# A decoder layer on one core: block sums loaded a tile ahead of their making, residual tiles loaded one a row block, half rows' statistics taken early

## The chip, the cores and the metric

The kernel runs on one core of a Trainium2 chip. The metric is the device time of one execution in microseconds (us). Each kernel is executed several times and the median counts. A profile is one further execution under the hardware profiler; its times are read from the start of its span.

Engines are named as in the profile: PE is the matrix engine (PEld its weight loads), DVE the vector engine, ACT the scalar engine, POOL GpSimd, SP SyncE, which here only issues DMAs. Each engine works through its own queue of instructions in order. In the listings of the timeline, a row is: start in us, duration in us, engine, source line, operation, destination and sources, count, and in brackets the idle time ahead of it with the instruction that ended that idle time.

## The reference, cut to what matters

One layer of a hybrid decoder in float32, for 1024 rows of width 1024. Two SwiGLU feed-forward networks (FFN1 and FFN2, hidden width 2816) stand around a token mixer. The change lies in the two feed-forward networks and their layer norms alone.

```python
def layer_norm(x, g, b, eps=LN_EPS):
    xf = x.astype(jnp.float32)
    mu = jnp.mean(xf, axis=-1, keepdims=True)
    var = jnp.mean(jnp.square(xf - mu), axis=-1, keepdims=True)
    return ((xf - mu) * lax.rsqrt(var + eps) * g + b).astype(x.dtype)

def swiglu(x, w_gate, w_up, w_down):
    return (jax.nn.silu(x @ w_gate) * (x @ w_up)) @ w_down

...
x = layer_norm(ALPHA * x + 0.5 * swiglu(x, ffn1_w_gate, ffn1_w_up, ffn1_w_down), ln1_g, ln1_b)
x = layer_norm(ALPHA * x + token_mixer(x, ...), ln2_g, ln2_b)
x = layer_norm(ALPHA * x + 0.5 * swiglu(x, ffn2_w_gate, ffn2_w_up, ffn2_w_down), ln3_g, ln3_b)
```

## The kernel before

**Arithmetic.** Every float32 operand of a product is split into a high and a low part (`split`: ACT casts the high part, L134, and POOL or DVE subtracts to get the low part, L138), and a product of 128x128 by 128x512 is three matmuls on PE: high by high, high by low, low by high (`mm3`, L154). The 2x2 block products of the feed-forward networks go by a scheme of seven products in place of eight.

**The gate half.** A loop over f = 0 to 21 (`gate_rest`) takes 128 columns of the gate and up weights at a time. One block is seven products of 12 matmuls of width 512; between them DVE adds the results (L291 and others) and the hidden rows h are stored to DRAM.

**Block sums.** The down half also needs sums and differences of quarters of its two operands. `sums` makes them ahead, in the gate loop: four 128x512 tiles are loaded (L388) into a ring of four buffers named `pr`, four additions or subtractions on DVE follow (L390 to L393 for kind "h", quarters of the hidden rows; L396 to L399 for kind "w", quarters of w_down), and the four results go to DRAM (L402). The blocks f = 0 to 10 each make one "w" sum, the blocks f = 12 to 21 one "h" sum, and `down_seven` makes the last "h" sum at its start.

**The down half.** `down_seven` runs seven products m = 0 to 6 of 11 row blocks i. For each block `part_load` (L418) loads two 128x512 tiles into a ring of eight buffers `rw`, both are split into a ring of fourteen buffers `wr` (here DVE makes the low parts), and PE runs 12 matmuls: three for each of four accumulators j. Products m = 0, 2, 3, 4 gather in the PSUM banks c, c, a, d, products 1, 5, 6 in g, g, b, b. At the end of product 0 DVE scales the residual tiles and adds the accumulators (12 instructions, L461); later products add theirs (L466). The eight residual tiles `u` (128x1024, from x or from x2) are loaded at block 3 of product 0 (L447), all at one place, right behind `hooks[0]`, which loads the layer norm's gain and bias (`lng`, `lnb`, L194). After product 4 the layer norms of row tiles 0 to 3 are handed out over the following blocks, and those of tiles 4 to 7 come after product 6. `layer_norm` takes two `bn_stats` a tile (L523, one for each half of the row), then an aggregate, a scale and a shift.

**What sets the order.** The order on each engine's queue is not that of the program text: a list scheduler places instructions at build time, with the program's order as the priority and the rings' buffers as limits. A load into a ring waits until the buffer's last reader is done; for `pr` this is the store at L402.

Of the kernel before, what the change touches and what calls it, by code (L numbers as in the profile page):

```python
# [16 lines left out]
P = 128  # L17
# [5 lines left out]
NH = NF // 2  # L23
# [8 lines left out]
class Net:  # L32
    def __init__(self, ctx, tc, ins, out):
        self.ctx, self.tc, self.nc, self.I, self.out = ctx, tc, tc.nc, ins, out
        tp = lambda **kw: ctx.enter_context(tc.tile_pool(**kw))
        self.cp = tp(name="cp", bufs=1)
        self.gp = {}
        self.sp = self.rp = self.ep = self.wp = None
        self.pp = tp(name="pp", bufs=1, space=PSUM)
        self.dp = tp(name="dp", bufs=1, space=bass.MemoryType.DRAM)  # L40
        self.n = 0
        self.SD = {}


    def nm(self, s):
# [280 lines left out]
    def gate_first(self, pre, src, cmb, hD):  # L326

        nc = self.nc
# [15 lines left out]
        for _ in steps:  # L344
            pass
        self.gate_up(cmb, 0, ws, hD, 256, 512)
        self.sums(pre, "w", self.I[f"{pre}_w_down"][0], 0)
        return self.gate_rest(pre, cmb, hD, 1)

    def gate_rest(self, pre, cmb, hD, f0):  # L350

        wd = self.I[f"{pre}_w_down"][0]
        for f in range(f0, NF):
            ws = self.weights(*(self.raws(pre, f, 0) + self.raws(pre, f, 1)))
            if f == NF - 1:
                self.down_parts(pre, hD)
                ahead = [self.part_load(0, i) for i in range(2)]
            if f == 0:
                self.gate_up(cmb, f, ws, hD, 0, 256)
                self.gate_up(cmb, f, ws, hD, 256, 512)  # L360
            else:
                self.gate_up(cmb, f, ws, hD)
            if f < NH:
                self.sums(pre, "w", wd, f)
            elif f > NH:
                self.sums(pre, "h", hD, f - NH - 1)
        return ahead


# [6 lines left out]
            r, c = c, r  # L376
        return src[(r * NH + i) * P:(r * NH + i + 1) * P, c * 512:(c + 1) * 512]

    def sums(self, pre, kind, src, i):

        nc = self.nc
        tt_ = nc.vector.tensor_tensor
        key = pre + kind
        if key not in self.SD:
            self.SD[key] = self.dram("sum_" + key, 4 * NH * P, 512)
        q11, q12, q21, q22 = (self.ring("pr") for _ in range(4))
        for t, r, c in ((q11, 0, 0), (q12, 0, 1), (q21, 1, 0), (q22, 1, 1)):
            nc.sync.dma_start(t, self.quarter(src, kind, r, c, i))  # L388
        if kind == "h":
            tt_(q22, q21, q22, op=ALU.add)  # L390
            tt_(q21, q11, q21, op=ALU.subtract)  # L391
# [29 lines left out]
    def down_seven(self, pre, src, hD, ln_cb, hooks, ahead):  # L421

        nc = self.nc
        stt, tt_ = nc.vector.scalar_tensor_tensor, nc.vector.tensor_tensor
        y, late, ahead = [], [], list(ahead)
        self.sums(pre, "h", hD, NH - 1)
        acc = {}
        for m in range(7):
            name = "XYXZZYY"[m]
# [4 lines left out]
            for i in range(NH):  # L434
# [4 lines left out]
                for t in raws:  # L439
                    d = self.ring("wr"), self.ring("wr")  # L440
                    self.split(t, *d, lo_eng="dve")
                    ds.append(d)
                if (m, i) == (0, 3):
                    hooks[0]()
                    for tt in range(8):
                        t = self.unit()
                        nc.sync.dma_start(t, src[tt * P:(tt + 1) * P, :])  # L447
                        y.append(t)
                if (m, i) == (5, 0):
                    hooks[1]()  # L450
                if i % 5 == 4 and late:
                    late.pop(0)()
                for j in range(4):
# [2 lines left out]
            for j in range(4):  # L456
# [5 lines left out]
                elif m == 2:  # L462
                    stt(c11, c11, ALPHA, ps[j], op0=ALU.mult, op1=ALU.add)
                else:
                    t = {1: c12, 3: c22, 4: c12, 5: c22, 6: c21}[m]
                    tt_(t, t, ps[j], op=ALU.add)  # L466
                if m == 4:
                    late.append(lambda tt=j: ln_cb(tt, y))
        for j in range(4):
# [46 lines left out]
    def layer_norm(self, tt, y, gb, bb, then):  # L516

        nc = self.nc
        if tt % 2 == 0:
            self.mv = self.s("lnmv", [P, 2, 2], bufs=2)  # L520
        st = self.s("lnst", [P, 2, 6], bufs=2)
        for i in range(2):
            nc.vector.bn_stats(st[:, i], y[tt][:, i * 512:(i + 1) * 512])  # L523
        nc.vector.bn_aggr(self.mv[:, tt % 2], st)
        nb = self.s("lnn", [P, 1], bufs=2)
# [898 lines left out]
```

## Time and profile before

| | |
|---|---|
| median of 3 runs | 3321.55 us (3304.94 to 3331.37) |
| the profiled execution's own time | 3326.53 us |
| its span | 3324.7 us |
| DVE busy | 62% of the span |
| mean granted PE clock | 0.955 |

The span is from the first to the last instruction; 1.83 us of the profiled execution lie outside it. The profiled execution is 5 us longer than the median. On this time scale FFN1's gate half runs from about 24 to 505 us, its down half to 753, the mixer and its output product follow, FFN2's gate half runs from about 2570 to 3078, its down half to 3304, and the last layer norm and the stores of the output end the span.

### The profile page before, as it was taken

What the parts mean: (1) busy time and instruction counts of PE and PEld (TensorE: products, weight loads), DVE (VectorE), ACT (ScalarE), POOL (GpSimd) and SP (SyncE); (2) the same over time, 40 slices, a digit from 0 to 9 for tenths busy, and PEclk for the clock granted to TensorE, in tenths of its full rate; (3) what the DMA queues carried; (4) which work ended last, traced back from release to release, by engine and by line L of the source; (5) the groups of instructions that cost most, each with busy time, mean ns of one, the idle gap of its engine ahead of it and who ended that gap; (6) DMA issues with size and microseconds to landing.
All of it is one profiled execution on the core that took longest, in us unless ns stands there. A gap on an engine that the chain in (4) does not pass through costs nothing. (4 is left out here: it accounts for less than half of the span.)

```text
span 3324.7 us, 45401 instructions
## 1 busy us (share of the span) xinstructions
PE 3054.4 (92%) x15624; PEld 2474.3 (74%) x15624; DVE 2048.0 (62%) x4940; ACT 1067.3 (32%) x1750; POOL 778.6 (23%) x819
## 2 busy tenths in 40 slices
PE   7899897998899999999999999989999789989897
PEld 6687776876677777787877777767777678767686
DVE  8644554574647766757576766366649754455557
ACT  4232222453312222313132222276434323222343
POOL 4444430011212222222222122100000344443000
PEclk9999998999989999999999999999999799999999
DMA  6734556662222322322222232375586563455764
GB/s 217 244 93 129 168 162 228 193 207 76 59 61 62 79 74 58 78 63 73 65 73 68 74 87 78 106 233 162 173 265 203 191 216 87 128 162 175 243 197 159
DMA packets 535405, 454.55 MB, mean 137 GB/s; under 512 B 115165, under 2 KB 403079, under 8 KB 535175
## 3 DMA queue, kind: packets, MB, share of 16 engines
q1 hardware_dynamic: 526151, 438.02, 43.5%
q0 software_dynamic: 4608, 8.39, 0.9%
q10 hardware_dynamic: 4416, 5.24, 0.5%
q8 instruction: 123, 2.02, 0.3%
q14 instruction: 107, 0.88, 0.1%
HBM read 322.03 MB, written 129.50 MB: 136 GB/s over the span
## 5 line engine op out<-in xcount | busy, mean ns | idle before, releaser
L154 PE MATMUL psg<-xT,wf 128*128 128x512 f32 x2352 | 640.2, 408 | 2.2 <-ACT f L968 1.2
L154 PEld LDWEIGHTS psg<-xT,wf 128*128 128x128 f32 x2352 | 429.8, 192 | 79.2 <-ACT f L968 1.6
L134 ACT CAST wr<-rw 128x512 fp32r<-128x512 f32 x488 | 288.7, 621 | 521.9 <-PE psg L154 167.1
L138 DVE TENSOR_TENSOR wr<-rw,wr 128x512 fp32r<-128x512 f32 x356 | 237.2, 697 | 185.1 <-ACT wr L134 183.1
L154 PE MATMUL psb<-xq,wr 128*128 128x512 f32 (+1 forms) x1104 | 280.9, 406 | 63.8 <-DVE e L291 61.8
L138 POOL TENSOR_TENSOR wr<-tw,wr 128x512 fp32r<-128x512 f32 x176 | 242.9, 1382 | 356.5 <-ACT wr L134 348.4
L154 PE MATMUL psa<-xT,w 128*128 128x512 f32 x1200 | 317.8, 407 | 8.3 <-DVE pj L604 4.6
L154 PEld LDWEIGHTS psb<-xq,wr 128*128 128x128 f32 x1104 | 213.0, 201 | 119.9 <-DVE e L291 75.1
L138 POOL TENSOR_TENSOR wr<-rw,wr 128x512 fp32r<-128x512 f32 x132 | 180.3, 1368 | 423.3 <-ACT wr L134 417.7
L154 PE MATMUL psc<-xq,wr 128*128 128x512 f32 (+1 forms) x1104 | 262.8, 387 | 4.8 <-DVE e L291 4.8
L154 PEld LDWEIGHTS psa<-xT,w 128*128 128x128 f32 x1200 | 222.4, 191 | 59.4 <-DVE pj L604 9.4
L154 PEld LDWEIGHTS psc<-xq,wr 128*128 128x128 f32 x1104 | 206.9, 194 | 47.3 <-DVE e L291 4.4
L134 ACT CAST wr<-tw 128x512 fp32r<-128x512 f32 x176 | 109.1, 621 | 397.2 <-PE psb L154 304.6
L291 DVE TENSOR_TENSOR e<-psb,e 128x512 f32<-128x512 f32 (+1 forms) x138 | 91.7, 665 | 187.0 <-PE psb L154 187.0
L154 PE MATMUL psc<-wr,wr 128*128 128x512 f32 x624 | 164.4, 398 | 28.3 <-ACT wr L134 27.8
L138 POOL TENSOR_TENSOR w<-raw,w 128x512 fp32r<-128x512 f32 (+1 forms) x51 | 65.6, 1302 | 491.2 <-PE psb L154 246.2
L138 POOL TENSOR_TENSOR wf<-rawf,wf 128x512 fp32r<-128x512 f32 x98 | 130.3, 1345 | 164.2 <-ACT wf L134 138.8
L154 PEld LDWEIGHTS psc<-wr,wr 128*128 128x128 f32 x624 | 118.8, 191 | 55.9 <-ACT wr L134 29.1
L154 PE MATMUL psg<-wr,wr 128*128 128x512 f32 x540 | 144.3, 396 | 7.6 <-DVE wr L138 6.9
L882 POOL TENSOR_SCALAR S<-S,PC 128x128 f32<-128x128 f32 x120 | 80.5, 671 | 296.5 <-DVE S L884 188.8
L154 PE MATMUL psb<-wr,wr 128*128 128x512 f32 x540 | 143.9, 395 | 0.0
L134 ACT CAST wf<-rawf 128x512 fp32r<-128x512 f32 x122 | 73.4, 619 | 196.0 <-PE psg L154 117.0
(368 smaller groups left out, 5472.1 us busy)
## 6 DMA issues: line engine op xcount, KB each, us to landing
rawf<-in_w_in_dram SPq DMA_DIRECT2D x98, 256.0 KB, 3.1
rw<-in_ffn_w_gate_dram SPq DMA_DIRECT2D x88, 256.0 KB, 3.0
rw<-in_ffn_w_up_dram SPq DMA_DIRECT2D x88, 256.0 KB, 3.1
pr<-in_ffn_w_down_dram SPq DMA_DIRECT2D x88, 256.0 KB, 4.2
pr<-h SPq DMA_DIRECT2D x88, 256.0 KB, 3.7
h<-e SPq DMA_DIRECT2D x80, 256.0 KB, 2.8
rw<-h SPq DMA_DIRECT2D x66, 256.0 KB, 3.5
rw<-in_ffn_w_down_dram SPq DMA_DIRECT2D x66, 256.0 KB, 3.2
```

The costliest lines, as they stand in the source:

```text
L134: nc.scalar.copy(hi, src)
L138: eng.tensor_tensor(lo, src, hi.bitcast(F32), op=ALU.subtract)
L154: self.nc.tensor.matmul(out, a[u], b[v], start=first and i == 0, stop=last and i == 2, skip_group_check=more)
L291: add = lambda o, a, b: nc.vector.tensor_tensor(o, a[:, cs], b, op=ALU.add)
L882: nc.gpsimd.tensor_scalar(S1, S, pcn, None, op0=ALU.mult)
```

## The change

`sums` is cut in two: `sums_load` issues the four loads of a sum, `sums_make` does the additions and the stores. In the program's text a sum's making now stands one block behind its loads (`self.pend` carries it over). The last "h" sum is loaded at block 1 of product 0 and made at block 7. The eight residual tiles are loaded one a block, at blocks 2 to 9 of product 0. The loads of the layer norm's gain and bias move from product 0, block 3, to product 1, block 3. After product 5 DVE takes `bn_stats` of the right half rows of tiles 4 to 7, which are final there, and `layer_norm` later takes only the left halves of these. The ring for the statistics has 6 buffers in place of 2.

```diff
--- before.py
+++ after.py
@@ -39,7 +39,7 @@
         self.pp = tp(name="pp", bufs=1, space=PSUM)
         self.dp = tp(name="dp", bufs=1, space=bass.MemoryType.DRAM)
         self.n = 0
-        self.SD = {}
+        self.SD, self.early, self.pend = {}, {}, None
 
 
     def nm(self, s):
@@ -344,7 +344,7 @@
         for _ in steps:
             pass
         self.gate_up(cmb, 0, ws, hD, 256, 512)
-        self.sums(pre, "w", self.I[f"{pre}_w_down"][0], 0)
+        self.pend = self.sums_load(pre, "w", self.I[f"{pre}_w_down"][0], 0)
         return self.gate_rest(pre, cmb, hD, 1)
 
     def gate_rest(self, pre, cmb, hD, f0):
@@ -360,10 +360,13 @@
                 self.gate_up(cmb, f, ws, hD, 256, 512)
             else:
                 self.gate_up(cmb, f, ws, hD)
+            if self.pend:
+                self.sums_make(*self.pend)
+                self.pend = None
             if f < NH:
-                self.sums(pre, "w", wd, f)
+                self.pend = self.sums_load(pre, "w", wd, f)
             elif f > NH:
-                self.sums(pre, "h", hD, f - NH - 1)
+                self.pend = self.sums_load(pre, "h", hD, f - NH - 1)
         return ahead
 
 
@@ -376,16 +379,21 @@
             r, c = c, r
         return src[(r * NH + i) * P:(r * NH + i + 1) * P, c * 512:(c + 1) * 512]
 
-    def sums(self, pre, kind, src, i):
+    def sums_load(self, pre, kind, src, i):
+
+        ts = [self.ring("pr") for _ in range(4)]
+        for t, (r, c) in zip(ts, ((0, 0), (0, 1), (1, 0), (1, 1))):
+            self.nc.sync.dma_start(t, self.quarter(src, kind, r, c, i))
+        return pre, kind, i, ts
+
+    def sums_make(self, pre, kind, i, ts):
 
         nc = self.nc
         tt_ = nc.vector.tensor_tensor
         key = pre + kind
         if key not in self.SD:
             self.SD[key] = self.dram("sum_" + key, 4 * NH * P, 512)
-        q11, q12, q21, q22 = (self.ring("pr") for _ in range(4))
-        for t, r, c in ((q11, 0, 0), (q12, 0, 1), (q21, 1, 0), (q22, 1, 1)):
-            nc.sync.dma_start(t, self.quarter(src, kind, r, c, i))
+        q11, q12, q21, q22 = ts
         if kind == "h":
             tt_(q22, q21, q22, op=ALU.add)
             tt_(q21, q11, q21, op=ALU.subtract)
@@ -423,7 +431,6 @@
         nc = self.nc
         stt, tt_ = nc.vector.scalar_tensor_tensor, nc.vector.tensor_tensor
         y, late, ahead = [], [], list(ahead)
-        self.sums(pre, "h", hD, NH - 1)
         acc = {}
         for m in range(7):
             name = "XYXZZYY"[m]
@@ -440,14 +447,15 @@
                     d = self.ring("wr"), self.ring("wr")
                     self.split(t, *d, lo_eng="dve")
                     ds.append(d)
-                if (m, i) == (0, 3):
-                    hooks[0]()
-                    for tt in range(8):
-                        t = self.unit()
-                        nc.sync.dma_start(t, src[tt * P:(tt + 1) * P, :])
-                        y.append(t)
-                if (m, i) == (5, 0):
-                    hooks[1]()
+                if m == 0 and 2 <= i < 10:
+                    t = self.unit()
+                    nc.sync.dma_start(t, src[(i - 2) * P:(i - 1) * P, :])
+                    y.append(t)
+                if (m, i) in ((0, 1), (0, 7)):
+                    self.sums_make(*self.pend)
+                    self.pend = self.sums_load(pre, "h", hD, NH - 1) if i == 1 else None
+                if (m, i) in ((1, 3), (5, 0)):
+                    hooks[m // 5]()
                 if i % 5 == 4 and late:
                     late.pop(0)()
                 for j in range(4):
@@ -464,6 +472,9 @@
                 else:
                     t = {1: c12, 3: c22, 4: c12, 5: c22, 6: c21}[m]
                     tt_(t, t, ps[j], op=ALU.add)
+                if m == 5:
+                    self.early[4 + j] = self.s("lnst", [P, 2, 6], bufs=6)
+                    nc.vector.bn_stats(self.early[4 + j][:, 1], c22)
                 if m == 4:
                     late.append(lambda tt=j: ln_cb(tt, y))
         for j in range(4):
@@ -518,8 +529,11 @@
         nc = self.nc
         if tt % 2 == 0:
             self.mv = self.s("lnmv", [P, 2, 2], bufs=2)
-        st = self.s("lnst", [P, 2, 6], bufs=2)
-        for i in range(2):
+        st = self.early.pop(tt, None)
+        part = range(2) if st is None else range(1)
+        if st is None:
+            st = self.s("lnst", [P, 2, 6], bufs=self.UB - 2)
+        for i in part:
             nc.vector.bn_stats(st[:, i], y[tt][:, i * 512:(i + 1) * 512])
         nc.vector.bn_aggr(self.mv[:, tt % 2], st)
         nb = self.s("lnn", [P, 1], bufs=2)
```
Since a scheduler places the instructions, the engines' queues show what the change moves. Names carry a running number; `h_77` and `h_78` are the hidden rows in DRAM, `sum_ffn1h` and `sum_ffn2h` the sums made from them.

**The start of product 0.** SP's queue in FFN1, before, from the last stores of the last "h" sum on: the eight residual tiles `u`, then the two `rw` tiles of block 4.

```order
L402 DMA sum_ffn1h<-pr_4110 128x512
L402 DMA sum_ffn1h<-pr_4111 128x512
L447 DMA u_4210<-in_x_dram 128x1024
L447 DMA u_4212<-in_x_dram 128x1024
L447 DMA u_4214<-in_x_dram 128x1024
L447 DMA u_4216<-in_x_dram 128x1024
L447 DMA u_4218<-in_x_dram 128x1024
L447 DMA u_4220<-in_x_dram 128x1024
L447 DMA u_4222<-in_x_dram 128x1024
L447 DMA u_4224<-in_x_dram 128x1024
L418 DMA rw_4238<-h_77 128x512
L418 DMA rw_4239<-in_ffn_w_down_dram 128x512
```
After, the same stretch, behind the four `pr` loads of the last sum:

```order
L452 DMA u_4174<-in_x_dram 128x1024
L452 DMA u_4200<-in_x_dram 128x1024
L426 DMA rw_4214<-h_77 128x512
L426 DMA rw_4215<-in_ffn_w_down_dram 128x512
L452 DMA u_4226<-in_x_dram 128x1024
L426 DMA rw_4240<-h_77 128x512
L426 DMA rw_4241<-in_ffn_w_down_dram 128x512
L452 DMA u_4252<-in_x_dram 128x1024
L426 DMA rw_4266<-h_77 128x512
L426 DMA rw_4267<-in_ffn_w_down_dram 128x512
L452 DMA u_4278<-in_x_dram 128x1024
L426 DMA rw_4292<-h_77 128x512
```
The `rw` tiles of block 4 stand behind two residual tiles in place of eight, and those of blocks 5 to 7 follow in turn; the stores of the last sum have moved behind block 7's tiles, and `lng` and `lnb`, which stood ahead of the stores, to product 1. In FFN2 the tiles of blocks 2 to 7 are already loaded ahead of this. SP's queue before, from the last sum's stores on, with block 8's `rw` tiles last:

```order
L402 DMA sum_ffn2h<-pr_26622 128x512
L402 DMA sum_ffn2h<-pr_26624 128x512
L402 DMA sum_ffn2h<-pr_26623 128x512
L447 DMA u_26724<-x2D 128x1024
L447 DMA u_26726<-x2D 128x1024
L447 DMA u_26728<-x2D 128x1024
L447 DMA u_26730<-x2D 128x1024
L447 DMA u_26732<-x2D 128x1024
L447 DMA u_26734<-x2D 128x1024
L447 DMA u_26736<-x2D 128x1024
L418 DMA rw_26846<-h_78 128x512
L418 DMA rw_26847<-in_ffn_w_down_dram 128x512
```
After, the same stretch:

```order
L452 DMA u_26686<-x2D 128x1024
L452 DMA u_26712<-x2D 128x1024
L452 DMA u_26738<-x2D 128x1024
L452 DMA u_26764<-x2D 128x1024
L452 DMA u_26790<-x2D 128x1024
L452 DMA u_26816<-x2D 128x1024
L410 DMA sum_ffn2h<-pr_26657 128x512
L410 DMA sum_ffn2h<-pr_26654 128x512
L410 DMA sum_ffn2h<-pr_26656 128x512
L410 DMA sum_ffn2h<-pr_26655 128x512
L426 DMA rw_26838<-h_78 128x512
L426 DMA rw_26839<-in_ffn_w_down_dram 128x512
```
Six residual tiles now stand ahead of the four stores and two behind block 8's tiles; before, seven stood between the stores and block 8.

**The end of product 0.** DVE's queue in FFN2, before: the low parts of product 1's blocks 0 and 1 (L138), then the scaling of the residual tiles from product 0's accumulators.

```order
L138 TENSOR_TENSOR wr_26939<-rw_26934,wr_26938 128x512
L138 TENSOR_TENSOR wr_26943<-rw_26935,wr_26942 128x512
L138 TENSOR_TENSOR wr_26963<-rw_26958,wr_26962 128x512
L138 TENSOR_TENSOR wr_26967<-rw_26959,wr_26966 128x512
L461 SCALAR_TENSOR_TENSOR u_26722<-u_26722,psc_26638 128x512
L461 SCALAR_TENSOR_TENSOR u_26730<-u_26730,psc_26638 128x512 x2
L461 SCALAR_TENSOR_TENSOR u_26724<-u_26724,psc_26639 128x512
L461 SCALAR_TENSOR_TENSOR u_26732<-u_26732,psc_26639 128x512 x2
L461 SCALAR_TENSOR_TENSOR u_26726<-u_26726,psa_26640 128x512
L461 SCALAR_TENSOR_TENSOR u_26734<-u_26734,psa_26640 128x512 x2
L461 SCALAR_TENSOR_TENSOR u_26728<-u_26728,psd_26641 128x512
L461 SCALAR_TENSOR_TENSOR u_26736<-u_26736,psd_26641 128x512 x2
```
After, the same stretch (L469 is the former L461):

```order
L138 TENSOR_TENSOR wr_26935<-rw_26930,wr_26934 128x512
L469 SCALAR_TENSOR_TENSOR u_26686<-u_26686,psc_26614 128x512
L469 SCALAR_TENSOR_TENSOR u_26790<-u_26790,psc_26614 128x512 x2
L469 SCALAR_TENSOR_TENSOR u_26712<-u_26712,psc_26615 128x512
L469 SCALAR_TENSOR_TENSOR u_26816<-u_26816,psc_26615 128x512 x2
L469 SCALAR_TENSOR_TENSOR u_26738<-u_26738,psa_26616 128x512
L469 SCALAR_TENSOR_TENSOR u_26850<-u_26850,psa_26616 128x512 x2
L469 SCALAR_TENSOR_TENSOR u_26764<-u_26764,psd_26617 128x512
L469 SCALAR_TENSOR_TENSOR u_26876<-u_26876,psd_26617 128x512 x2
L138 TENSOR_TENSOR wr_26939<-rw_26931,wr_26938 128x512
L138 TENSOR_TENSOR wr_26959<-rw_26954,wr_26958 128x512
```
Only one of the four low parts still stands ahead of the scaling; the other operand of block 0 and both of block 1 come behind it. FFN1 has the same order after, and before had three ahead of the scaling. PE's queue at product 1's block 0, before:

```order
L154 MATMUL psg_26930<-wr_26942,wr_26938 128x512
L154 MATMUL psg_26930<-wr_26943,wr_26938 128x512
L154 MATMUL psg_26930<-wr_26942,wr_26939 128x512
L154 MATMUL psg_26931<-wr_26942,wr_26938 128x512
L154 MATMUL psg_26931<-wr_26943,wr_26938 128x512
L154 MATMUL psg_26931<-wr_26942,wr_26939 128x512
L154 MATMUL psb_26932<-wr_26942,wr_26938 128x512
L154 MATMUL psb_26932<-wr_26943,wr_26938 128x512
L154 MATMUL psb_26932<-wr_26942,wr_26939 128x512
L154 MATMUL psb_26933<-wr_26942,wr_26938 128x512
L154 MATMUL psb_26933<-wr_26943,wr_26938 128x512
L154 MATMUL psb_26933<-wr_26942,wr_26939 128x512
```
After:

```order
L154 MATMUL psg_26926<-wr_26938,wr_26934 128x512
L154 MATMUL psg_26927<-wr_26938,wr_26934 128x512
L154 MATMUL psb_26928<-wr_26938,wr_26934 128x512
L154 MATMUL psb_26929<-wr_26938,wr_26934 128x512
L154 MATMUL psg_26926<-wr_26939,wr_26934 128x512
L154 MATMUL psg_26926<-wr_26938,wr_26935 128x512
L154 MATMUL psg_26927<-wr_26939,wr_26934 128x512
L154 MATMUL psg_26927<-wr_26938,wr_26935 128x512
L154 MATMUL psb_26928<-wr_26939,wr_26934 128x512
L154 MATMUL psb_26928<-wr_26938,wr_26935 128x512
L154 MATMUL psb_26929<-wr_26939,wr_26934 128x512
L154 MATMUL psb_26929<-wr_26938,wr_26935 128x512
```
The four high-by-high matmuls of the block now go first, and the fifth needs `wr_26939`, the low part that DVE makes behind the scaling.

**The "w" sums.** DVE's queue in FFN2 at the fifth "w" sum (`e` are the gate half's additions), before:

```order
L291 TENSOR_TENSOR e_23185<-psb_23190,e_23182 128x512
L269 TENSOR_TENSOR tw_23480<-rw_23476,rw_23472 128x512
L396 TENSOR_TENSOR pr_23786<-pr_23787,pr_23786 128x512
L291 TENSOR_TENSOR e_23186<-psc_23191,e_23185 128x512
L269 TENSOR_TENSOR tw_23481<-rw_23474,tw_23479 128x512
L397 TENSOR_TENSOR pr_23787<-pr_23789,pr_23787 128x512
```
After (L404 is the former L396):

```order
L291 TENSOR_TENSOR e_23176<-psb_23181,e_23173 128x512
L269 TENSOR_TENSOR tw_23472<-rw_23468,rw_23464 128x512
L291 TENSOR_TENSOR e_23177<-psc_23182,e_23176 128x512
L404 TENSOR_TENSOR pr_23786<-pr_23787,pr_23786 128x512
L269 TENSOR_TENSOR tw_23473<-rw_23466,tw_23471 128x512
L291 TENSOR_TENSOR e_23178<-psb_23181,e_23173 128x512
```
One addition more (L291) stands ahead of the sum's first subtraction, whose tiles a DMA brings. Of the 22 "w" sums, 10 have moved back, past up to three such additions or up to five weight subtractions (L269), and 12 stand where they stood. Of the 22 "h" sums none has moved among the additions and weight subtractions of DVE, and SP's queue from block 12 to the last stores of the gate loop has the same order before and after, in both networks.

## The prediction

> **What bounds the kernel now.** I read the page's busy times first, then the waits, then PE in slices of 25 us, then the timeline of the slices in which PE stands.
>
> ```profile
> span 3324.7 us, 45401 instructions
> PE 3054.4 (92%) x15624; PEld 2474.3 (74%) x15624; DVE 2048.0 (62%) x4940; ACT 1067.3 (32%) x1750; POOL 778.6 (23%) x819
> ...
> 175.00:275.00 100.00, 100.00 (x443) 82.84 (x442) 40.93 (x57) 31.57 (x53) 47.79 (x37) 1.00 0.31 87
> 300.00:500.00 200.00, 181.88 (x763) 146.61 (x762) 107.83 (x134) 51.43 (x86) 80.69 (x59) 0.97 0.53 166
> 525.00:550.00 25.00, 15.44 (x56) 12.27 (x57) 9.02 (x14) 8.30 (x14) 0.00 (x0) 0.73 0.88 315
> 2860.00:3070.00 210.00, 190.05 (x794) 153.62 (x793) 110.61 (x135) 56.55 (x95) 84.69 (x63) 0.96 0.53 166
> 3100.00:3125.00 25.00, 13.03 (x48) 10.01 (x47) 10.01 (x16) 7.77 (x13) 0.00 (x0) 0.73 0.88 327
> ```
>
> PE bounds the kernel: between 175 and 275 us it is never idle, at full clock (the columns behind a window's length are the busy times of PE, PEld, DVE, ACT and POOL, then granted clock, DMA share and GB/s). So only what stops PE counts. It stops at the two seams between gate half and down half (9.6 and 12.0 us idle in 25, the DMA engines 88% busy), and in the "h" sum stretches: 200 − 181.88 = 18.1 us and 210 − 190.05 = 20.0 us idle. There the clock of 0.97 and 0.96 takes another 200 × 0.03 + 210 × 0.04 = 14 us, so about 52 us are lost in these two.
>
> The seam of FFN1, PE first, then SP's issues, then DVE:
>
> ```profile
> 508.21 0.50 PE L154 MATMUL psc<-wr,wr 128*128 128x512 f32 x1 [3.29 <-ACT wr L134]
> ...
> 521.14 0.84 PE L154 MATMUL psd<-wr,wr 128*128 128x512 f32 x3
> 534.56 3.23 PE L154 MATMUL psc<-wr,wr 128*128 128x512 f32 x6 [12.58 <-ACT wr L134]
> 537.59 1.48 PE L154 MATMUL psa<-wr,wr 128*128 128x512 f32 x3
> 538.87 1.39 PE L154 MATMUL psd<-wr,wr 128*128 128x512 f32 x3
> 540.10 1.55 PE L154 MATMUL psc<-wr,wr 128*128 128x512 f32 x6
> ...
> 556.46 1.52 PE L154 MATMUL psg<-wr,wr 128*128 128x512 f32 x6
> ...
> 562.89 1.24 PE L154 MATMUL psg<-wr,wr 128*128 128x512 f32 x4 [2.64 <-DVE wr L138]
> ...
> 590.98 1.52 PE L154 MATMUL psc<-wr,wr 128*128 128x512 f32 x6
> ...
> 510.30 0.43 SPq L194 DMA_DIRECT2D lng<-in_ln_g_dram  x1
> ...
> 518.93 4.08 SPq L447 DMA_DIRECT2D u<-in_x_dram  x8
> 523.13 0.63 SPq L418 DMA_DIRECT2D rw<-h  x1
> ...
> 515.19 0.69 DVE L390 TENSOR_TENSOR pr<-pr,pr 128x512 f32<-128x512 f32 x1 [3.81 <-issue]
> ...
> 554.98 3.67 DVE L461 SCALAR_TENSOR_TENSOR u<-u,psc 128x512 f32<-128x512 f32 x6
> 558.56 1.88 DVE L461 SCALAR_TENSOR_TENSOR u<-u,psa 128x512 f32<-128x512 f32 x3
> 560.35 1.88 DVE L461 SCALAR_TENSOR_TENSOR u<-u,psd 128x512 f32<-128x512 f32 x3
> 562.15 3.10 DVE L138 TENSOR_TENSOR wr<-rw,wr 128x512 fp32r<-128x512 f32 x5
> ```
>
> The reader sees a chain: SP waits for the last "h" sum to store it, issues eight residual tiles, and only then block 4's `rw`; PE stands 12.58 us, and the matmuls after the gap are slow: block 4 takes 540.10 − 534.56 = 5.54 us. The same in FFN2, at block 8:
>
> ```profile
> 3099.78 0.84 PE L154 MATMUL psd<-wr,wr 128*128 128x512 f32 x3
> 3112.59 3.23 PE L154 MATMUL psc<-wr,wr 128*128 128x512 f32 x6 [11.97 <-ACT wr L134]
> ...
> 3123.13 1.52 PE L154 MATMUL psg<-wr,wr 128*128 128x512 f32 x6
> 3124.49 1.52 PE L154 MATMUL psb<-wr,wr 128*128 128x512 f32 x6
> 3125.85 1.52 PE L154 MATMUL psg<-wr,wr 128*128 128x512 f32 x6
> ...
> 3153.88 1.52 PE L154 MATMUL psc<-wr,wr 128*128 128x512 f32 x6
> ...
> 3086.59 0.43 SPq L194 DMA_DIRECT2D lnb<-in_ln_b_dram  x1
> ...
> 3091.78 0.69 DVE L390 TENSOR_TENSOR pr<-pr,pr 128x512 f32<-128x512 f32 x1 [3.58 <-DMA pr<-h]
> ...
> 3097.43 3.99 SPq L447 DMA_DIRECT2D u<-x2D  x7
> 3101.52 0.51 SPq L418 DMA_DIRECT2D rw<-h  x1
> ```
>
> An undisturbed block is 3125.85 − 3123.13 = 2.72 us, so a product of 11 is 29.92 us.
>
> **The "h" stretches: 0.** The queues of SP and DVE there have the same order before and after, and `pr` still holds one sum: its next loads wait for the last stores. What is named as a load one tile ahead does not take place there.
>
> **Residual tiles, FFN1.** Block 3 ends at 521.14 + 0.84 = 521.98. Without a stall the seven blocks left would end at 541.0; product 0 ends at 556.46, so 15.4 us is the most to be had and 0 the least (all waits for data move, none goes). After, two tiles and block 4's `rw` are issued from 510.3 on: 1.05 + 0.52 MB, at 315 GB/s 5 us, so block 4 comes about in time. Before block 8 lie six tiles of 0.52 MB, ten `rw` and four sum stores of 0.26 MB: 3.15 + 2.62 + 1.05 = 6.8 MB, 21.7 us from 510.3, and some 2 us of the `pr` loads' rest: 534. With 1.3 us for cast and split and about 1 us to landing (both estimates from the first `rw` issue to PE's start, 523.13 to 534.56, which also held 4 MB of tiles) it starts at 536.5; PE would reach it at 521.98 + 4 × 2.72 = 532.9. A stall of 3.6 us and 2 us of slow clock put the end at 546.7: **−9.5** (rounded; 0 to −15.4).
>
> **Residual tiles, FFN2.** PE reaches block 8 at 3100.62; it starts at 3112.59. After, six tiles are issued ahead of the stores, right behind the last `pr` loads (from 3086.2, where `lng` stood), and so move while DVE still waits for its tiles at 3091.78. The stores and block 8's `rw` follow by 3098, with 1.05 + 0.52 MB left to move, 5 us, plus 2.3 us: 3105.3. With 1.8 us of slow clock and three blocks product 0 ends at 3115.2: **−7.9** (0 to −14.3, no stall at all).
>
> **The scaling ahead of the low parts: a new wait.** The 12 scalings take 562.15 − 554.98 = 7.2 us. Before, block 0 of product 1 had its low parts ahead of them. After, one low part of block 0 stands behind them: PE runs four matmuls, 0.9 us, and then waits. The first scaling can start when the sixth matmul of the last block is done, 1.1 us ahead of the product's end; so the low part is there 7.2 + 0.7 − 1.1 = 6.8 us into product 1, near 7.0 with the hand-over, and PE idles 6.1 us. The slow clock after it lies between the gap of 2.64 us (the 12 matmuls from 562.89 to block 2 ran some 1.75 us long) and that of 12.58 us (5.54 − 2.72 = 2.8): I take 2.0, so product 1 takes 38.0 us. It took 590.98 − 556.46 = 34.5 in FFN1 and 3153.88 − 3123.13 = 30.75 in FFN2: **+3.5** and **+7.3** (together between +5, if product 0's last block hides more, and +13).
>
> [...]
>
> **Statistics and layer norm.** By DVE's queue seven `bn_stats` run behind product 6 in FFN2 before, four after; two rows of that stretch:
>
> ```profile
> 3305.44 1.28 DVE L523 BATCH_NORM_STATS2 lnst<-u 128x6 f32<-128x512 f32 x2
> ...
> 3318.28 2.48 DVE L537 SCALAR_TENSOR_TENSOR u<-u,lnr,lnb 128x1024 f32<-128x1024 f32 x2
> ```
>
> DVE is the path there, at 0.6 us for one: 3 × 0.6 = 1.8 at most, **−1.5** in each network since ACT's shifts also wait; −3 in all (0 to −3.6). The early ones lie ahead of low parts at product 6's start, 4 × 0.6 = 2.4 us where a block lead of `wr` buffers covers; and the layer norms of tiles 2 and 3 come later there: **+1** (0 to +4). Gain and bias loads amid product 1, on a queue that then has slack: 0 (to +3).
>
> **The "w" sums.** Two of the waits that stop PE by a sum's tiles:
>
> ```profile
> 94.57 0.69 DVE L397 TENSOR_TENSOR pr<-pr,pr 128x512 f32<-128x512 f32 x1 [4.67 <-issue]
> ...
> 98.34 4.35 PE L154 MATMUL psb<-xq,wr 128*128 128x512 f32 x12 [3.75 <-DVE e L291]
> ...
> 2647.54 1.41 DVE L396 TENSOR_TENSOR pr<-pr,pr 128x512 f32<-128x512 f32 x1 [3.82 <-DMA pr<-in_ffn_w_down_dram]
> 2649.61 4.53 PE L154 MATMUL psc<-xq,wr 128*128 128x512 f32 x12 [3.03 <-DVE e L291]
> ```
>
> Both belong to sums that move behind the next addition. Idle 3.75 + 3.03, and slow clock 4.35 + 4.53 − 2 × 2.88 = 3.1 (12 matmuls at 0.24): 9.9 us at most. The tile's wait stays and can meet the next addition, so I take half: **−5** (+4 to −10).
>
> **Sum.** −9.5 − 7.9 + 3.5 + 7.3 − 3 + 1 − 5 = −13.6 us against the profiled execution's 3326.5, so 3313. That execution lies 5 us above the median of the runs, 3321.55; from the median the sum gives 3308. I forecast 3310.
>
> **Rivals.** *Slower:* the new wait at product 1 comes in any case (+10.8), but product 0 gains little. For it: in FFN2 six tiles go into the queue before the sum is made, so the `pr` tiles may land late, the stores hold SP, and block 8's `rw` waits again. Against it: at 3086.59 1 MB of gain and bias stood behind the same loads and DVE waited only 3.58 us. If both gains are lost, −3 + 1 − 5 + 10.8 = +4, and +9 if the "w" waits only move: 3326 to 3331 from the median. It decides where the two gains make less than 10.8 − 7 = 3.8 us.
>
> *The seams go entirely:* −15.4 − 14.3 + 10.8 − 3 + 1 − 10 = −31, so 3291. For it: the 315 GB/s are a mean, and some of it is stores; against it the 6.8 MB ahead of block 8 in FFN1.
>
> *The "h" waits go too,* as the change's words say: −52 more at most, near 3256 with the forecast's other terms. Only for it: a shift of the same queue by some us against the stores. Against it stands the unchanged order.
>
> *Nothing to be seen:* the parts cancel within 4 us, 3318 to 3325. For it: every gain here is a wait for data that the same DMA engines must bring.
>
> **Chances.** Forecast (3300 to 3317) 0.48, seams gone 0.16, "h" waits gone 0.06, nothing 0.15, slower 0.15. A measurement of this kernel tells about 1% from no change, 33 us; faster by more than that (under 3288.3) needs the "h" waits or a little over the seams: 0.06 + 0.04 = 0.10; slower by more (over 3354.8) has no mechanism here that reaches it: 0.03; within 1% 0.87. The range 3288 to 3329 leaves out the "h" case, the best of the seams and the worst of the slower case.
>
> **What would show it.** In the changed profile: block 4 of FFN1 without a long gap; a gap of 3 to 6 us at block 8 of each product 0; a gap near 6 us with a low part of DVE as its releaser 0.9 us into each product 1; waits of PE for L291 in the "h" stretches unchanged, near 38 us idle; four `bn_stats` in the tail. I am wrong if the gap in product 1 is missing, if a residual tile is late for the scaling, or if the "h" stretches get shorter by more than 10 us.

## The result, and the profile after

| | before | after |
|---|---|---|
| median of 15 runs | 3316.46 us (3304.32 to 3331.37) | 3295.53 us (3285.8 to 3313.7) |
| ratio of the times | | 0.9943, 95% interval 0.9925 to 0.9962 |
| the profiled execution's span | 3324.7 us | 3284.1 us |

The change is 0.6% faster: 18.9 us by the ratio (12.6 to 24.9). The two profiled executions, of 3326.5 and 3285.8 us, lie further apart than the medians, 40.6 us by their spans. 12.8 us of this lie between FFN1's last down product and FFN2's first gate block (1879.6 us before, 1866.8 after), where both kernels have the same instructions but for the early statistics in the first layer norm; in the other profiles below this stretch takes 1849 to 1876 us. So spans are not compared here, only stages.

All stage times come from the timeline's rows: a gate block by the product of its gated halves on DVE (L319), a down product from its first matmul to the next one's. Two numbers are FFN1 / FFN2, in us. The tail is from the end of PE's last matmul to the span's end. An undisturbed stretch of ten blocks is 190.4 us, an undisturbed product 29.92 us; where an edit moves DVE's own instructions, the marks of the blocks move with them by up to 3 us.

| kernel | blocks 1-10 | blocks 12-21 | product 0 | product 1 | products 5+6 | tail |
|---|---|---|---|---|---|---|
| before | 209.6 / 208.0 | 217.0 / 219.9 | 48.2 / 44.6 | 34.5 / 30.8 | 70.0 / 60.0 | 21.1 |
| after | 207.1 / 203.4 | 216.8 / 217.5 | 33.0 / 32.4 | 37.7 / 37.6 | 71.8 / 60.0 | 19.1 |
| e1 residual tiles only | 210.7 / 208.2 | 216.8 / 218.8 | 38.6 / 39.5 | 37.3 / 35.4 | 70.0 / 60.0 | 21.2 |
| e1b the same, gain and bias moved | 211.9 / 206.3 | 212.4 / 212.1 | 37.5 / 36.7 | 37.4 / 38.2 | 69.4 / 60.0 | 21.2 |
| e2 after without e1b's part | 208.4 / 203.1 | 217.3 / 218.4 | 44.5 / 40.8 | 34.5 / 30.7 | 72.2 / 60.0 | 19.1 |
| e4 early statistics only | 210.4 / 206.3 | 220.7 / 213.7 | 48.1 / 42.8 | 34.4 / 30.8 | 71.6 / 60.0 | 19.1 |
| e5 two blocks split first | 208.2 / 203.5 | 220.7 / 204.8 | 33.4 / 35.2 | 36.4 / 33.6 | 71.5 / 60.0 | 19.2 |
| e10 scaling handed out | 210.1 / 204.9 | 215.8 / 212.9 | 33.2 / 34.8 | 30.0 / 30.0 | 71.9 / 60.0 | 19.1 |
| e7 making held back | 189.4 / 188.9 | 190.7 / 190.4 | 34.2 / 36.5 | 38.1 / 37.6 | 72.0 / 60.0 | 20.0 |
| e12 e7 and e10 | 189.4 / 188.9 | 191.3 / 190.1 | 34.1 / 35.4 | 30.0 / 30.0 | 71.6 / 60.0 | 19.3 |
| e13 before, held in its block | 187.7 / 192.2 | 189.3 / 189.3 | 49.0 / 45.0 | 34.5 / 30.8 | 67.1 / 60.0 | 21.1 |

The seams after the change, PE's timeline, FFN1 and then FFN2:

```profile
504.92 3.30 PE L154 MATMUL psc<-wr,wr 128*128 128x512 f32 x6 [3.30 <-ACT wr L134]
...
529.78 0.62 PE L154 MATMUL psc<-wr,wr 128*128 128x512 f32 x2
...
537.94 0.62 PE L154 MATMUL psg<-wr,wr 128*128 128x512 f32 x2
538.39 0.61 PE L154 MATMUL psb<-wr,wr 128*128 128x512 f32 x2
544.70 2.07 PE L154 MATMUL psg<-wr,wr 128*128 128x512 f32 x4 [5.69 <-DVE wr L138]
...
575.61 1.52 PE L154 MATMUL psc<-wr,wr 128*128 128x512 f32 x6
...
3069.22 0.73 PE L154 MATMUL psc<-wr,wr 128*128 128x512 f32 x2 [2.06 <-ACT wr L134]
...
3077.51 0.62 PE L154 MATMUL psg<-wr,wr 128*128 128x512 f32 x2
...
3084.27 2.08 PE L154 MATMUL psg<-wr,wr 128*128 128x512 f32 x4 [5.69 <-DVE wr L138]
...
3115.15 1.52 PE L154 MATMUL psc<-wr,wr 128*128 128x512 f32 x6
```

The gaps of 12.6 and 12.0 us in product 0 are gone; 2.06 us at block 8 of FFN2 is what is left of them. In their place PE runs four matmuls of product 1 and stands 5.69 us in both networks. DVE's timeline of FFN1 shows for what, and SP's how the tiles now come:

```profile
536.78 3.67 DVE L469 SCALAR_TENSOR_TENSOR u<-u,psc 128x512 f32<-128x512 f32 x6 [0.53 <-PE psc L154]
540.37 1.88 DVE L469 SCALAR_TENSOR_TENSOR u<-u,psa 128x512 f32<-128x512 f32 x3
542.17 1.87 DVE L469 SCALAR_TENSOR_TENSOR u<-u,psd 128x512 f32<-128x512 f32 x3
543.96 3.09 DVE L138 TENSOR_TENSOR wr<-rw,wr 128x512 fp32r<-128x512 f32 x5
...
507.00 0.91 SPq L452 DMA_DIRECT2D u<-in_x_dram  x2
508.00 0.41 SPq L426 DMA_DIRECT2D rw<-h  x1
...
518.43 2.95 SPq L410 DMA_DIRECT2D sum_ffn1h<-pr  x4
522.40 0.32 SPq L426 DMA_DIRECT2D rw<-h  x1
```

The first low part of the five at 543.96 is the one that PE needs: it stands behind all 12 scalings. The lists of waits (total, times, longest) and two windows over the "h" blocks tell what has not changed. The waits before, then after:

```profile
PE psb L154 <- DVE e L291: 64.2, 32, 4.0
DVE pr L390 <- DMA pr<-h: 64.7, 21, 5.0
DVE pr L396 <- DMA pr<-in_ffn_w_down_dram: 37.3, 13, 5.3
...
PE psb L154 <- DVE e L291: 62.9, 34, 3.8
DVE pr L398 <- DMA pr<-h: 60.8, 21, 5.1
DVE pr L404 <- DMA pr<-in_ffn_w_down_dram: 43.1, 14, 5.1
```

The windows after, with the columns of the prediction's, which shows those before:

```profile
300.00:500.00 200.00, 182.78 (x774) 147.96 (x775) 105.91 (x132) 51.08 (x86) 78.63 (x58) 0.97 0.52 165
2825.00:3035.00 210.00, 191.84 (x804) 155.20 (x803) 112.53 (x138) 57.10 (x97) 87.28 (x65) 0.96 0.53 165
```

PE still stands 17 and 18 us in these windows, the clock is still 0.97 and 0.96, and DVE waits for the sums' tiles as long as before (104 us in these two rows, 102 before). A load one tile ahead did not come about in the gate loop.

### The profile page after: what moved, and what is told of

Same layout as the page of the kernel before. It is cut to its first block, busy times and chain, and to the rows that moved or that the text cites. A ratio compares the mean times of both kernels' runs of the same rounds, so it can differ in the third digit from the quotient of the medians.

```text
span 3284.1 us, 45405 instructions
## 1 busy us (share of the span) xinstructions
PE 3035.6 (92%) x15624; PEld 2456.9 (75%) x15624; DVE 2051.9 (62%) x4940; ACT 1066.5 (32%) x1750; POOL 779.6 (24%) x819
## 5 line engine op out<-in xcount | busy, mean ns | idle before, releaser
L138 DVE TENSOR_TENSOR wr<-rw,wr 128x512 fp32r<-128x512 f32 x356 | 238.0, 697 | 162.6 <-ACT wr L134 161.4
L138 POOL TENSOR_TENSOR wr<-tw,wr 128x512 fp32r<-128x512 f32 x176 | 243.1, 1382 | 353.9 <-ACT wr L134 348.2
L138 POOL TENSOR_TENSOR wr<-rw,wr 128x512 fp32r<-128x512 f32 x132 | 178.9, 1357 | 416.7 <-ACT wr L134 411.1
L291 DVE TENSOR_TENSOR e<-psb,e 128x512 f32<-128x512 f32 (+1 forms) x138 | 91.7, 664 | 184.1 <-PE psb L154 184.1
L138 POOL TENSOR_TENSOR w<-raw,w 128x512 fp32r<-128x512 f32 (+1 forms) x51 | 66.6, 1318 | 471.9 <-ACT w L134 410.7
L138 POOL TENSOR_TENSOR wf<-rawf,wf 128x512 fp32r<-128x512 f32 x98 | 131.3, 1355 | 164.9 <-ACT wf L134 150.0
```

The source lines that it names most:

```text
L138: eng.tensor_tensor(lo, src, hi.bitcast(F32), op=ALU.subtract)
L291: add = lambda o, a, b: nc.vector.tensor_tensor(o, a[:, cs], b, op=ALU.add)
```

## The experiments

**The residual tiles alone.** The kernel before, with the residual tiles spread (e1), then also with the gain and bias loads moved (e1b).

```diff
+                if m == 0 and 2 <= i < 10:
+                    t = self.unit()
+                    nc.sync.dma_start(t, src[(i - 2) * P:(i - 1) * P, :])
+                    y.append(t)
                 if (m, i) == (0, 3):
                     hooks[0]()
-                    for tt in range(8):
-                        t = self.unit()
-                        nc.sync.dma_start(t, src[tt * P:(tt + 1) * P, :])
-                        y.append(t)
```

In e1b `hooks[0]` runs at `(m, i) == (1, 3)`.

> The kernel before with one part of the change: the eight residual tiles are loaded one a block at blocks 2 to 9 of product 0 (gain and bias stay at block 3, sums and statistics as before). Theory (the spread of the residual tiles makes the gain, and itself moves the scaling ahead of product 1's low parts): product 0 falls from 48.2 to 36-39 us in FFN1 and from 44.6 to 33-36 in FFN2, product 1 rises to 37-38 in FFN1 and 33-35 in FFN2, in all 15 to 20 us less than before, ratio 0.994 to 0.9955. Rival (the gain needs the last sum to be made later, since its stores hold SP): product 0 of FFN1 stays over 44 us and the ratio over 0.997.

> The kernel before with the residual tiles spread and the loads of gain and bias moved to product 1 (sums and statistics as before). Theory (of the 5.5 to 7 us by which product 0 stays above the changed kernel when only the residual tiles are spread, the gain and bias loads ahead of block 4 or 8, 1 MB or some 2.6 us, are a part and the stores of the last sum ahead of the tiles the rest): product 0 at 35-37.5 us in both networks. Rival (gain and bias cost nothing there): 38.5 and 39.5 us as without them moved.

e1: ratio 0.9969 (0.9949 to 0.9988), less gain than the expected 0.994 to 0.9955, though the interval reaches into it; product 0 falls to 38.6 as expected and to 39.5, where 33 to 36 were expected; product 1 rises to 37.3 and 35.4. The rival, by which FFN1's product 0 stays over 44, falls. e1b, one run of 3288.28 us beside a median of 3308.64 for the kernel before: product 0 at 37.5 and 36.7, as its theory has it. SP's queue of e1 in FFN1 shows what is still ahead of block 4:

```profile
510.35 0.91 SPq L445 DMA_DIRECT2D u<-in_x_dram  x2
515.02 2.98 SPq L402 DMA_DIRECT2D sum_ffn1h<-pr  x4
518.04 0.43 SPq L194 DMA_DIRECT2D lng<-in_ln_g_dram  x1
518.52 0.46 SPq L194 DMA_DIRECT2D lnb<-in_ln_b_dram  x1
519.08 0.38 SPq L418 DMA_DIRECT2D rw<-h  x1
```

SP is ready at 511.3 and then waits 3.8 us for DVE to make the last sum, in order to store it. So product 0's gain has three parts, FFN1 / FFN2: the residual tiles 9.7 / 5.1 us (48.2 to 38.6, 44.6 to 39.5), gain and bias 1.1 / 2.8, and the last sum's stores behind the tiles 4.5 / 4.3 (37.5 to 33.0, 36.7 to 32.4). These are differences of single profiles, and part of each is slow clock: of the 4.5 us by which e1b's product 0 in FFN1 is longer than the changed kernel's only 1.5 are idle, and block 5 there takes 529.36 − 524.40 = 4.96 us, 0.23 of them idle, where an undisturbed block takes 2.72. In FFN2, where product 0 differs by up to 3 us between kernels with the same order of instructions, the last two parts are not told apart. Spreading the residual tiles also makes product 1's wait by itself.

**The change without them.** e2 is the changed kernel with residual tiles, gain and bias all at block 3 of product 0 again; the split sums and the early statistics stay.

> The changed kernel without that part: residual tiles and gain and bias all at block 3 of product 0 again; the split sums and the early statistics stay. Theory: the gap of product 0 comes back for the most part, 40 to 46 us in FFN1 (the stores of the last sum no longer stand ahead of block 4) and 42 to 45 in FFN2; product 1 falls back to 31-35 us; about 6 to 12 us less than before, ratio 0.9965 to 0.998. Rival (the sums made later are what removes the gap): product 0 stays at 33-36 us and the ratio below 0.995.

Ratio 0.9952 (0.9934 to 0.9971), a little better than expected. Product 0 is at 44.5 and 40.8 us (40 to 46 and 42 to 45 were expected), so most of the gap is back, product 1 at its old 34.5 and 30.7. The gain lies elsewhere: blocks 1 to 10 are 1.1 and 4.9 us shorter, product 0 is 3.7 and 3.8 shorter by the sum made later, the tail 2.0. The changed kernel, at 0.9943, is not told apart from e2: of the 19.9 us that the residual part takes off the two products 0 it puts 10.1 on the two products 1. The rival, by which the sums alone remove the gap, falls.

**The early statistics alone.** e4 is the kernel before with `bn_stats` of the right halves taken after product 5.

```diff
+                if m == 5:
+                    self.early[4 + j] = self.s("lnst", [P, 2, 6], bufs=6)
+                    nc.vector.bn_stats(self.early[4 + j][:, 1], c22)
```

> The kernel before with the early statistics alone. Theory (three of them leave DVE's tail, and the layer norms of tiles 2 and 3 land among the splits of product 6): from PE's end to the span's end 19.1 us in place of 21.1; products 5 and 6 of FFN1 about 72 us in place of 70.0, those of FFN2 unchanged at 60.0; products 0 and 1 as before (48, 34.5, 44.6, 30.75), the sum within 4 us of nothing. Rival (the 2 us more in FFN1's products 5 and 6 come from the other parts of the change): these stay at 70.

One run, 3312.08 us beside one of 3302.62, which tells no difference. By stages it is as the theory has it: tail 19.1, FFN1's products 5 and 6 at 71.6, products 0 and 1 as before but for FFN2's product 0, which is 1.9 us shorter with the same order of instructions. The rival, by which products 5 and 6 stay at 70, falls. In the changed kernel the layer norm of tiles 2 and 3 stands among the low parts of product 6 (DVE, then PE):

```profile
721.34 2.32 DVE L551 SCALAR_TENSOR_TENSOR u<-u,lnr,lnb 128x1024 f32<-128x1024 f32 x1
723.58 1.75 DVE L138 TENSOR_TENSOR wr<-rw,wr 128x512 fp32r<-128x512 f32 x1
...
725.39 2.04 PE L154 MATMUL psg<-wr,wr 128*128 128x512 f32 x5 [2.79 <-DVE wr L138]
```

**Two blocks split first.** e5 is the changed kernel; the splits of product 1's blocks 0 and 1 come ahead of the scaling in the text.

```diff
+            if m == 0:
+                cut = [self.split2(self.part_load(m + 1, i)) for i in range(2)]
             for j in range(4):
                 c11, c12 = (y[j][:, c * 512:(c + 1) * 512] for c in range(2))
```

> The changed kernel; in the program's text the first two blocks of product 1 are loaded and split ahead of the scaling of the residual tiles, so that their low parts no longer stand behind the 12 scalings on DVE. Theory (the low part behind the scaling is the new wait of 5.7 us with the slow clock after it): product 1 falls from 37.7 to 30-32 us in both networks, 12 to 15 us below the changed kernel, ratio to the kernel before 0.989 to 0.991. Rival (the split tiles are late for another reason, the loads from the sums): a gap over 3 us remains at product 1 and the ratio stays over 0.992.

Ratio 0.9907 (0.9885 to 0.9929), as the theory has it, but not by its mechanism: product 1 takes 36.4 and 33.6 us, not 30 to 32. That gives 1.3 and 4.1 us of the 12 by which the ratio lies below the changed kernel's; the two intervals overlap, and where the rest comes from is open. PE and DVE of FFN1:

```profile
548.94 0.39 PE L154 MATMUL psg<-wr,wr 128*128 128x512 f32 x1
552.58 2.50 PE L154 MATMUL psg<-wr,wr 128*128 128x512 f32 x5 [3.26 <-DVE wr L138]
...
545.86 1.88 DVE L479 SCALAR_TENSOR_TENSOR u<-u,psc 128x512 f32<-128x512 f32 x3
547.65 1.88 DVE L479 SCALAR_TENSOR_TENSOR u<-u,psa 128x512 f32<-128x512 f32 x3
549.45 1.88 DVE L479 SCALAR_TENSOR_TENSOR u<-u,psd 128x512 f32<-128x512 f32 x3
551.24 3.70 DVE L138 TENSOR_TENSOR wr<-rw,wr 128x512 fp32r<-128x512 f32 x6
```

The wait has moved to block 2, whose low parts stand behind the nine scalings that are left. The rival is right that a gap stays, and wrong in its reason: DVE ends it, not a load. The profile's blocks 12 to 21 of FFN2 happen to be 13 us shorter than in the changed kernel, with the same order of instructions there; so much these stretches scatter. The ratio alone would have confirmed the wrong story.

**The scaling handed out.** e10 is the changed kernel with two scalings a block, from block 1 of product 1 on.

```diff
                 if m == 0:
-                    for t in (c12, c21, c22):
-                        stt(t, t, ALPHA, ps[j], op0=ALU.mult, op1=ALU.add)
+                    scale += [lambda t=t, p=ps[j]: stt(t, t, ALPHA, p, op0=ALU.mult, op1=ALU.add) for t in (c12, c21, c22)]
...
+                for _ in range(2 if m == 1 and i else 0):
+                    if scale:
+                        scale.pop(0)()
```

> The changed kernel with the 12 scalings of product 0 handed out two a block behind the splits of product 1's blocks 1 to 6, in place of all at product 0's end (moving only the splits of two blocks ahead left a gap of 3.3 us at block 2, since nine scalings still stood there). Theory (the wait is DVE's 7.2 us of scaling in one piece): product 1 runs without a gap over 1 us, 30-31 us in both networks where the changed kernel needs 37.7, 12 to 14 us below it, ratio to the kernel before 0.988 to 0.992. Rival (product 1's tiles come late by themselves, since the loads of the sums follow ten tiles and the residuals): a gap over 2 us with a DMA or ACT behind it, product 1 over 33 us.

Ratio 0.9900 (0.9875 to 0.9924), product 1 at 30.05 us in both networks, with no gap, so the rival, by which its tiles come late, falls. DVE now takes scalings and low parts in turn, at 0.6 us each, 2.4 us of a block's 2.72:

```profile
545.22 0.68 DVE L471 SCALAR_TENSOR_TENSOR u<-u,psc 128x512 f32<-128x512 f32 x1
545.82 0.68 DVE L138 TENSOR_TENSOR wr<-rw,wr 128x512 fp32r<-128x512 f32 x1
546.42 0.68 DVE L471 SCALAR_TENSOR_TENSOR u<-u,psc 128x512 f32<-128x512 f32 x1
547.02 0.68 DVE L138 TENSOR_TENSOR wr<-rw,wr 128x512 fp32r<-128x512 f32 x1
```

**The making really held back.** e7 is the changed kernel; the first instruction of a sum's making also adds a zero column that is worked out from the next block's first addition `u2`, so no order can put it earlier.

```diff
             if self.pend:
-                self.sums_make(*self.pend)
+                self.sums_make(*self.pend, hold=self.u2)
                 self.pend = None
...
+            z = self.cp.tile([P, 1], F32, tag="hold", bufs=2, name=self.nm("hold"))
+            nc.vector.tensor_scalar(z, hold[:, 0:1], 0.0, None, op0=ALU.mult)
...
+        def first(o, a, b, op):
+            if z is None:
+                tt_(o, a, b, op=op)
+            else:
+                nc.vector.scalar_tensor_tensor(o, a, z, b, op0=ALU.add, op1=op)
...
-            tt_(q22, q21, q22, op=ALU.add)
+            first(q22, q21, q22, ALU.add)
...
-            tt_(q11, q12, q11, op=ALU.subtract)
+            first(q11, q12, q11, ALU.subtract)
```

> The changed kernel; the making of each sum in the gate loop is really held back by one block: its first instruction also adds a zero column worked out from the next block's first addition, so that the scheduler cannot place it earlier (22 sums a network, one small instruction more each for 20 of them). Theory (the split changed nothing in the order, DVE still waits for the tiles right behind their loads, and PE waits behind DVE): DVE's waits for the tiles of a sum fall from 104 us to under 20, PE's waits for the additions from 63 to under 30, blocks 12 to 21 fall from a mean of 22 to 19.5-20.5 us, 30 to 50 us below the changed kernel, ratio 0.979 to 0.986. Rival (the DVE work of a sum itself, not its wait, stops PE): blocks stay over 21.5 us and the ratio over 0.991.

Median 3196.24 us, ratio 0.9658 (0.9637 to 0.9679): twice what was expected, since blocks 1 to 10, which the expectation did not price, gave 18 and 15 us beside the 26 and 27 of blocks 12 to 21. These gains are against the changed kernel, 85 us in all of the 94 by which the two ratios differ. All four stretches stand at 189 to 191 us, PE without a gap; two windows:

```profile
300.00:450.00 150.00, 150.00 (x663) 124.20 (x662) 93.48 (x120) 44.77 (x75) 68.22 (x51) 1.00 0.60 192
2760.00:2940.00 180.00, 180.00 (x796) 149.05 (x795) 111.96 (x145) 56.03 (x94) 83.13 (x63) 1.00 0.59 187
```

And DVE's timeline at one "h" sum:

```profile
384.54 0.69 DVE L291 TENSOR_TENSOR e<-psb,e 128x512 f32<-128x512 f32 x1 [3.14 <-PE psb L154]
385.26 0.15 DVE L397 TENSOR_SCALAR hold<-e 128x1 f32<-128x1 f32 x1
385.45 1.39 DVE L403 SCALAR_TENSOR_TENSOR pr<-pr,hold,pr 128x512 f32<-128x512 f32 x1
```

And what is left in the list of waits:

```profile
DVE pr L401 <- DMA pr<-h: 4.9, 3, 2.8
...
PE psb L154 <- DVE e L291: 2.6, 3, 1.5
```

DVE now waits for PE at a sum and no longer for a DMA, but for 4.9 us at the last two sums of each network, which are made without a hold (another 3.5 us there end by nothing that the profile shows); PE's waits for the additions fall from 62.9 us to 2.6. The rival, that a sum's work stops PE and not its wait, falls: the work is the same, with a small instruction more.

**Held without the split.** e13 is the kernel before, with none of the change; the first instruction of a making adds a zero column from its own block's gated product, so that it stands late in the block.

```diff
-                self.sums(pre, "w", wd, f)
+                self.sums(pre, "w", wd, f, self.up1)
             elif f > NH:
-                self.sums(pre, "h", hD, f - NH - 1)
+                self.sums(pre, "h", hD, f - NH - 1, self.up1)
```

`sums` uses it as `sums_make` does in e7.

> The kernel before, with none of the change: loads and making of a sum stay in one block, only the first instruction of the making also adds a zero column worked out from the block's gated product, late in the same block, so that it stands behind the block's additions on DVE. Theory (what counts is where the making stands in DVE's queue against the landing of its tiles, some 5 us behind their issue, and not the split over two blocks): blocks 1-10 and 12-21 come to 19.0-19.8 us as with the split and hold, 75 to 95 us less than before, ratio 0.971 to 0.978. Rival (a block of lead is needed): blocks stay over 20.5 us and the ratio over 0.985.

Ratio 0.9727 (0.9705 to 0.9750), 90 us; the gate blocks at 187.7 to 192.2 us, the seams as before. DVE's waits for the tiles of a sum fall to 8.3 us, all at the sum without a hold, and PE's for the additions to 5.5. A lead of one block is not needed. What is needed is that the making stands behind its landed tiles.

**Both.** e12 is e7 with e10's edit.

> The changed kernel with both: sums made one block later by a real dependency, and the scalings handed out over product 1. Theory (the two costs lie in different stages and add): gate blocks stay at 19.04 us, product 1 at 30-31 us, ratio 0.961 to 0.963, about 3185 us. Rival (without the stalls of the gate half the seam's transfers pile up): products 0 and 1 together stay over 70 us and the ratio at 0.965 or more.

Median 3182.23 us, ratio 0.9615 (0.9592 to 0.9637): the gains add (14 us below e7, and 15.7 are off its products 1), and this kernel is 3.9% below the kernel before. Products 0 and 1 take 64 and 65 us together, so the rival falls.

## Why the prediction came out as it did

The median, 3295.5 us, lies in the range of 3288 to 3329 and 14 us under the forecast of 3310; 13.6 us of gain were summed, 18.9 measured. Another 5 of the 14 us are the base: the forecast started from 3321.55, the median of three runs, where 15 runs give 3316.46. The case that had the largest chance, 3300 to 3317, was missed. The nearest case is the rival by which the seams go entirely, 3291, and its argument, that the 315 GB/s are a mean, is what the runs bear out. Step by step, by stages:

- **The "h" stretches, 0.** Right: 217.0 to 216.8 and 219.9 to 217.5 us, waits as before. The rival by which these waits go was priced at 52 us; e7 took 55.8 us (217.0 + 219.9 − 190.7 − 190.4) there, so place and price were right, and that the change would not get it was read from the order. Over the four profiles with the split sums (after, e2, e5, e10) and the four without (before, e1, e1b, e4) the means differ by +0.9 and −2.7 us, against a scatter of 8 to 14 at the same order. What the prediction did not see is that the "w" blocks held another 39 us (209.6 + 208.0 − 189.4 − 188.9). It priced only two of their waits.
- **The residual tiles, −9.5 and −7.9.** Products 0 became 15.2 and 12.2 us shorter. In two kernels with the same order of loads up to there, e5 and e10, FFN1's product 0 is at 33.4 and 33.2, as here; FFN2's is at 35.2 and 34.8, and e4, with the order of before, has 42.8 there, so FFN2's gain is 8 to 12 and the forecast lies at its edge. FFN1's term was undersized, and was off most. The step that failed is "6.8 MB, 21.7 us from 510.3": the rate of 315 GB/s was the mean of 25 us in which the engines were full only for the first 10 (DMA share 1.03 at 405 GB/s, then 0.77 at 255). The two parts of that window before; then two windows after the change, the first with the queue filling (0.92), the second with it full (1.04); then ACT's cast of block 8's tiles:

```profile
525.00:535.00 10.00, 0.44 (x1) 0.29 (x1) 1.10 (x2) 1.64 (x3) 0.00 (x0) 0.57 1.03 405
535.00:550.00 15.00, 15.00 (x56) 11.98 (x56) 7.92 (x13) 6.66 (x12) 0.00 (x0) 0.83 0.77 255
...
507.00:517.00 10.00, 10.00 (x37) 8.06 (x37) 6.08 (x10) 2.39 (x4) 0.00 (x0) 0.80 0.92 332
517.00:527.00 10.00, 10.00 (x46) 8.29 (x45) 4.27 (x7) 3.72 (x6) 0.00 (x0) 1.00 1.04 399
...
528.27 1.28 ACT L134 CAST wr<-rw 128x512 fp32r<-128x512 f32 x2 [3.91 <-DMA rw<-h]
```

  The 20 us after have a mean of 366 GB/s, by which the 6.8 MB take 18.6 us, 3.1 less (17.1 at 399). Block 8's first tile has landed at 528.27; the prediction, on this time scale (3.3 us earlier than that of before), had it at 531.7. The difference is the stall of 3.6 us and with it its slow clock: block 8 begins at 529.78 without a gap, where a gap of 3 to 6 us was named as a sign. In FFN2 that gap is 2.06 us, below the sign too, where 4.7 were worked out. The prediction also named only the residual tiles for this gain; by e1, e1b and e2 some 8.8 us of it are the last sum made later and 3.9 the gain and bias.
- **The scaling ahead of the low parts, +3.5 and +7.3.** Right: +3.1 and +6.9. The gap is 5.69 us where 6.1 were forecast, and 37.67 − 29.92 − 5.69 = 2.06 us of slow clock follow it where 2.0 were taken; that this came so close is in part luck, since the same gap costs 1.7 to 2.5 us over the runs (last section). e10 shows the cause.
- **Statistics, −3 and +1.** Right within 1 us. The tail gave −2.0 in FFN2 and about as much ahead of the mixer (PE's wait for the first normed tile falls from 6.30 to 4.55 us); FFN1's products 5 and 6 took +1.8, which e4 shows to be theirs.
- **The "w" sums, −5.** −2.5 and −4.6 in the profile after, −1.1 and −4.9 in e2. The means of the same four profiles with the split and four without differ by 2.2 and 3.5 us, 5.7 in all. Only two waits were priced and half of them taken, where ten sums had moved, so that −5 came out near is in part luck.

Without the "h" stretches these terms sum to −26 us, somewhat beyond the measured interval's end of −24.9, as two single profiles can with blocks 12 to 21 that scatter by 8 us and more and FFN2's product 0 by 3. What makes these stretches and the mixer's differ between executions was not tried.

## What to carry to other kernels

Where a scheduler places instructions, a load written earlier in the text need not lead its use by anything: read from the queues whether the waiting instruction has moved, and if it has not, give it a dependency on something later; here one small instruction a sum took 95 us out of the gate loops, with the split (e7) and without it (e13), where the split in the text alone took 6 to 7. Whatever is moved off one point of a queue, ask who now stands in front of the next stage's first operand, and hand a long piece of work out in the steps at which the other engine consumes. And a ratio that comes out as expected does not show the mechanism: look at the stage.

## What the runs showed of the hardware

Gaps of the same length cost PE different amounts of slow clock. In e5, a gap of 3.26 us in FFN1's product 1 is followed by 36.41 − 29.92 − 3.26 = 3.2 us of loss, one of 3.27 us in FFN2's by 33.57 − 29.92 − 3.27 = 0.4. The granted clock (the third number from the end) over the 6.8 us behind each gap tells the same:

```profile
552.58:559.38 6.80, 6.80 (x17) 5.36 (x18) 3.65 (x6) 1.14 (x2) 0.00 (x0) 0.55 0.68 232
3079.12:3085.92 6.80, 6.80 (x30) 5.63 (x31) 5.06 (x9) 2.29 (x4) 0.00 (x0) 1.00 0.88 282
```

Before the change a gap of 2.64 us in product 1 cost 34.53 − 29.92 − 2.64 = 2.0, and three other runs with this gap agree within 0.1; the gap of 5.69 us, which stands in seven products 1 of the table, cost 1.7 to 2.5; and after the change one of 2.06 us cost 0.3, at a granted clock of 1.00. So the loss does not go by the length of the gap alone: the 3.2 us behind 3.26 us are more than any of the seven gaps of 5.69 us cost. What else sets it was not shown.
